# Building the S5 tables beside the FFN: output products on VectorE, a reordered table stage, paced gathers

## The chip, the cores and the metric

The kernel runs on one core of a Trainium2 chip. The metric is the device time of one execution in microseconds (us), the median of several runs. A core has five engines with their own instruction queues, each worked in order: TensorE (PE, with PEld for its weight loads), VectorE (DVE), ScalarE (ACT), GpSimd (POOL) and SyncE (SP), which here only issues DMAs. They meet through semaphores; data lie in SBUF (128 partitions) and in PSUM, into which TensorE writes.

## The reference

A decoder trunk of two layers with SEQ = 256 tokens and D_MODEL = 1024: in each layer a half-step SwiGLU FFN, a token mixer (layer 0: differential attention, layer 1: an S5 state-space block with GLU), a second half-step FFN, and a gated per-layer input (PLE). Every sub-layer has an RMSNorm before and behind it.

```
for i in range(DEPTH):
    x = x + 0.5 * rmsnorm(swiglu(rmsnorm(x, g[0]), ffn_w_in[i, 0], ffn_w_out[i, 0]), g[1])
    h = rmsnorm(x, g[2])
    m = diff_attention(h, ...) if i % 2 == 0 else s5_glu(h, ...)
    x = x + rmsnorm(m, g[3])
    x = x + 0.5 * rmsnorm(swiglu(rmsnorm(x, g[4]), ffn_w_in[i, 1], ffn_w_out[i, 1]), g[5])
    gate = sigmoid(rmsnorm(x, g[6]) @ ple_w_gate[i])
    x = x + rmsnorm(gate * (p[i] @ ple_w_proj[i]), g[7])
```

The S5 block is what the change is about. Each of 64 groups of 16 channels has 64 complex states, and the reference scans them:

```
lam_dt = lam * dt;  a_bar = exp(lam_dt);  b_bar = ((a_bar - 1) / lam) * b
a_pow  = exp(steps * lam_dt)
xs = associative_scan(a_bar, b_bar @ u) + a_pow * state
y  = real(c @ xs) + d_g * u
z  = gelu(y) @ w_glu + b_glu
```

The kernel doesn't scan token by token. It works in pieces of eight tokens with tables that depend only on the parameters: V (powers of a times b: from the inputs into the state), O (c times powers of a: from the state to the outputs), T (a block-Toeplitz table from inputs to outputs in one piece, the products c a^k b with d on its diagonal) and E (powers of a to the eighth, for the step from piece to piece).

## The kernel before

The 256 tokens are two row blocks of 128, worked by two threads (b = 0 and 1) whose steps alternate. The stages are ffn00, attn, ffn01, ple0, ffn10, ssm with GLU, ffn11, ple1. Matmuls keep fp32 accuracy by splitting: each product is a trio, hi*hi (L312), lo*hi (L313), hi*lo (L314). Weights come as blocks of 128x1024: SP loads raw (512 KB; three raw buffers), ACT rounds it to hi (L136), DVE subtracts to get lo (L138); nine pairs of hi and lo are held. Blocks are numbered in the order of their use: 100 to 143 are the first matrix of ffn01 (up), 144 to 165 its second (dn), 166 to 173 the PLE gate, 174 to 239 ffn10, and then come those of the S5 block.

Between two stages stand a post-norm (ygpn L383, the norm's factors v_pn and r_pn on POOL, x L387), then the transposes of x on PE (xT_ps, L349) with their split into xThi (ACT) and xTlo (DVE, L332).

The tables are built by a generator, ssm_tables, which thread b = 1 advances every few of its steps while ffn01, ple0 and the start of ffn10 run. Its parts are, in this order: a's powers and the complex multiplies (cmul, L717 to L726) of the E powers (10 of them, 60 DVE instructions, names cme, er, ei); b's and c's tables (names cmb, br, bi, cre, cim); and then for each of eight groups six POOL products of 128x512 for V (L907 to L912, names vr, vi, ptv), copies of c (cp), eight PE transposes (v_ps, L933) with an ACT copy and the store to v_d, eight small matmuls and a transpose for T (m_ps, L940 and L946), and six more POOL products for O (names or, oi, pto, in the same two buffers as vr and vi) with their stores o_d (L956). Then d is put on T's diagonal (db, dg, msb, L960 to L969), the pieces are stored to m_d (L972), and eight gathers of 512 KB in DRAM, issued by POOL, lay out the table t_d (L975).

Which instruction stands where on an engine is not decided by the chip: when the program is built, a scheduler plays the threads' steps through with priorities (the generator's steps get their own) and writes one order for each engine. On the chip every engine follows its list and waits where an input or a buffer isn't ready.

Of the kernel before, what the change touches and what calls it, by code (L numbers as in the profile page):

```python
# [9 lines left out]
F32 = mybir.dt.float32  # L10
# [3 lines left out]
ALU = mybir.AluOpType  # L14
AX = mybir.AxisListType

P = 128
# [50 lines left out]
          ("ffn", 1, 0), ("ssm",), ("ffn", 1, 1), ("ple", 1)]  # L68
TABLE_EVERY = OPT.get("every", 3)
PREPARE_AT = 36  # L70
EARLY = 24
# [76 lines left out]
def trunk(ctx, tc, x, p, norm_g, ffn_w_in, ffn_w_out, attn_w_qkv, attn_w_o, attn_lam, attn_subln_g,  # L148
# [136 lines left out]
    def flat(u):  # L285
        return [u] if isinstance(u, int) else [a for e in u for a in flat(e)]
# [479 lines left out]
    def ssm_tables(pool, keep):  # L766
# [61 lines left out]
        yield  # L828
        erf, eif = (t.rearrange("p g q j -> p (g q) j") for t in (er, ei))
        for m in (1, 2, 4, 8, 16):  # L830
            w = min(m, 31 - m)
            for h in range(2):
                sl = slice(16 * h, 16 * h + 16)
                b_r = erf[:, sl, m:m + 1].broadcast_to([P, 16, w])
                b_i = eif[:, sl, m:m + 1].broadcast_to([P, 16, w])
                cmul(v, pool, erf[:, sl, m + 1:m + w + 1], eif[:, sl, m + 1:m + w + 1], erf[:, sl, 1:w + 1], eif[:, sl, 1:w + 1],
                     b_r, b_i, [16, w], f"e{m}{h}")
            if m >= 4:
                yield

# [17 lines left out]
        for nm, src in (("re", ssm_b_re), ("im", ssm_b_im)):  # L858
            t = pool.tile([P, 32, 16], F32, tag="v" + nm[0], name=f"braw{nm}", bufs=1)
            nc.sync.dma_start(t, src[0].rearrange("(c e) p h -> (e p) c h", e=2))  # L860
            bb.append(t)
# [33 lines left out]
        cps = []  # L895
        for j in range(2):
# [6 lines left out]

        def products(out_r, out_i, ar_, ai_, br_, bi_, nm):
            g = nc.gpsimd
            t = pool.tile([P, 512], F32, tag="pt", name=f"pt{nm}", bufs=1).rearrange("p (q k h) -> p q k h", q=4, k=8)
# [7 lines left out]
        zt = pool.tile([16, 112], F32, tag="vr", name="zt", bufs=1)  # L914
        nc.gpsimd.memset(zt, 0.0)
        nc.gpsimd.dma_start(m_d[:, :, 0:7, :].rearrange("i g k o -> i g (k o)"),
                          zt.rearrange("p (o x) -> p o x", o=1).broadcast_to([16, 64, 112]))
        for gp in range(8):
            vr = pool.tile(shp, F32, tag="vr", name=f"vr{gp}", bufs=1)
            vi = pool.tile(shp, F32, tag="vi", name=f"vi{gp}", bufs=1)  # L920
            A = [t[:, :, gp, 0:8].broadcast_to(shp) for t in a4]
            B = [t[:, :, gp:gp + 1, :].broadcast_to(shp) for t in b4]
            products(vr, vi, *A, *B, f"v{gp}")
            for e in range(2):
                sl = slice(64 * e, 64 * e + 64)
                nc.gpsimd.tensor_copy(cps[0][sl, :, e, :], c_re[sl, :, gp, :])
                nc.gpsimd.tensor_scalar(cps[1][sl, :, e, :], c_im[sl, :, gp, :], -1.0, None, ALU.mult)
            for i in range(2):
# [9 lines left out]
            for ri in range(2):  # L938
                for q in range(4):
                    nc.tensor.matmul(mp[32 * q:32 * q + 32, 0:P], cps[ri][:, q].rearrange("p e h -> p (e h)"),  # L940
                                     (vr, vi)[ri][:, q].rearrange("p k h -> p (k h)"), start=ri == 0, stop=ri == 1,
                                     skip_group_check=True)
# [4 lines left out]
            nc.scalar.copy(msb[:, gp].rearrange("p e q h -> p q e h"), mp2[:, :P].rearrange("p (q e h) -> p q e h", q=4, e=2))  # L947
            yield
# [9 lines left out]
            yield  # L958

        m16 = msb.rearrange("p g e q h -> p (g e q) h")  # L960
        for q in range(4):
            db = pool.tile([16, 16, 16], F32, tag="cn", name=f"db{q}", bufs=1)
            nc.gpsimd.dma_start(db, ssm_d[:, 256 * q:256 * q + 256].rearrange("o (g h) -> o g h", h=16).broadcast_to([16, 16, 16]))
            dg = pool.tile([16, 16, 16], F32, tag="vi", name=f"dg{q}", bufs=1)
            nc.gpsimd.dma_start(dg, norm_g[1, 2:3, 256 * q:256 * q + 256].rearrange("o (g h) -> o g h", h=16).broadcast_to([16, 16, 16]))
            v.tensor_tensor(db, db, dg, ALU.mult)
            v.tensor_tensor(db, db, ident[0:16, 0:16].rearrange("p (o h) -> p o h", o=1).broadcast_to([16, 16, 16]), ALU.mult)
            mq = msb.rearrange("p g e q h -> p (g e) q h")[0:16, :, q, :]
            v.tensor_tensor(mq, mq, db, ALU.add)  # L969
        yield 1  # L970
        for k in range(8):
            nc.gpsimd.dma_start(m_d[:, :, 7 + k, :], m16[16 * k:16 * k + 16])  # L972
        yield 2
        for s_ in range(8):
            nc.gpsimd.dma_start(t_d[16 * s_:16 * s_ + 16].rearrange("i g (c x) -> i (g c) x", x=P),  # L975
                              m_d.rearrange("i g k o -> i g (k o)")[:, :, 16 * s_:16 * s_ + P])
            yield 2

# [309 lines left out]
    while any(s_ == "run" for s_ in state):  # L1288
# [16 lines left out]
        if started and b == 1 and steps[1] % pre["every"] == 0:  # L1305
            tables_step()
        if has_ssm and "pool" in ssm and ("V", 0) not in ssm and W.next >= plan[("ssm",)][0][0] - OPT["vl"]:
            load_v()
        if state == ["join", "join"]:
            end_tables()  # L1310
            if ("V", 0) not in ssm:
                load_v()
            pool = ssm["pool"]
# [30 lines left out]
```

## Time and profile before

| | us |
|---|---|
| median of 3 runs (lowest, highest) | 1120.79 (1118.37, 1122.93) |
| the profiled execution | 1120.96 |
| span from its first to its last instruction | 1119.2 |
| PE busy | 1043.0 (93%) |
| DVE busy | 696.5 (62%) |
| ACT busy | 553.8 (49%) |
| POOL busy | 255.4 (23%) |
| mean granted TensorE clock | 0.975 |

The profile is of one execution. Busy shares are averages over stages with different limits; POOL, for example, is busy 85 to 90% of the time from 420 to 616 us and hardly elsewhere. Times in the views are in us from the span's start. A view by windows gives the busy time of each engine in each stretch, with the granted clock (1.00 is full speed) and the DMA share. "Idle before" and "waited for" give idle time of an engine, put down to what ended it.

### The profile page before, as it was taken

How to read it: one execution, taken by the hardware profiler on the slowest of the kernel's cores; microseconds unless marked ns; L12 is line 12 of the kernel's file. 1: busy time of each engine (PE TensorE's matmuls, PEld its weight loads, DVE VectorE, ACT ScalarE, POOL GpSimd, SP SyncE). 2: the span in 40 equal slices, each digit the busy share in tenths (PEclk: the TensorE clock that was granted, in tenths of full speed). 3: DMA queues.
4: the chain of work that ended last, by engine and by line, in shares of the span. 5: the costliest groups of instructions: out<-in, count | busy, mean ns of one | idle time of the engine just before them, and what ended most of it. 6: DMA issues, size and time to landing. Idle time of an engine off the chain costs nothing. (4 is left out here: it accounts for less than half of the span.)

```text
span 1119.2 us, 14344 instructions
## 1 busy us (share of the span) xinstructions
PE 1043.0 (93%) x5123; PEld 835.7 (75%) x5123; DVE 696.5 (62%) x1011; ACT 553.8 (49%) x875; POOL 255.4 (23%) x315
## 2 busy tenths in 40 slices
PE   7999999999989999999778998999768899999996
PEld 5888888787766887777556886888546778888885
DVE  6656645688568986554686663654377676555464
ACT  6545444566655544443464543543335465444454
POOL 1002100100011018887788530000131010000001
PEclk9999999999999999999898999999989999999999
DMA  9656656476366777666564778766874647665651
GB/s 328 197 149 189 210 189 201 144 235 201 106 144 185 207 179 233 208 194 216 157 181 118 211 236 307 247 198 206 225 308 166 204 148 215 188 186 180 198 168 57
DMA packets 119816, 218.62 MB, mean 195 GB/s; under 512 B 25025, under 2 KB 43489, under 8 KB 119745
## 3 DMA queue, kind: packets, MB, share of 16 engines
q1 hardware_dynamic: 116864, 211.71, 60.9%
q0 software_dynamic: 1824, 5.33, 1.7%
q8 instruction: 40, 0.66, 0.2%
q10 hardware_dynamic: 1056, 0.66, 0.2%
q14 instruction: 32, 0.25, 0.1%
HBM read 205.13 MB, written 16.74 MB: 198 GB/s over the span
## 5 line engine op out<-in xcount | busy, mean ns | idle before, releaser
L138 DVE TENSOR_TENSOR lo<-raw,hi 128x1024 fp32r<-128x1024 f32 x332 | 429.6, 1301 | 266.3 <-ACT hi L136 264.7
L136 ACT CAST hi<-raw 128x1024 fp32r<-128x1024 f32 x332 | 347.3, 1052 | 327.1 <-PE up L314 106.5
L312 PE MATMUL up<-hi,xThi 128*128 128x512 f32 x704 | 279.3, 400 | 5.2 <-ACT hi L136 2.9
L313 PE MATMUL up<-lo,xThi 128*128 128x512 f32 x704 | 278.8, 397 | 1.5 <-DVE lo L138 1.4
L314 PE MATMUL up<-hi,xTlo 128*128 128x512 f32 x704 | 279.0, 400 | 0.0
L312 PEld LDWEIGHTS up<-hi,xThi 128*128 128x128 f32 x704 | 133.9, 190 | 34.8 <-ACT xThi L331 4.3
L313 PEld LDWEIGHTS up<-lo,xThi 128*128 128x128 f32 x704 | 134.1, 190 | 31.1 <-DVE lo L138 3.6
L314 PEld LDWEIGHTS up<-hi,xTlo 128*128 128x128 f32 x704 | 133.5, 191 | 28.1 <-issue 0.4
L312 PE MATMUL dn<-hi,hThi 128*128 128x512 f32 x352 | 139.2, 396 | 0.0
L313 PE MATMUL dn<-lo,hThi 128*128 128x512 f32 x352 | 138.5, 393 | 0.0
L314 PE MATMUL dn<-hi,hTlo 128*128 128x512 f32 x352 | 138.4, 394 | 0.0
L312 PEld LDWEIGHTS dn<-hi,hThi 128*128 128x128 f32 x352 | 66.8, 190 | 14.2 <-issue 0.6
L314 PEld LDWEIGHTS dn<-hi,hTlo 128*128 128x128 f32 x352 | 66.7, 190 | 14.3 <-issue 0.2
L313 PEld LDWEIGHTS dn<-lo,hThi 128*128 128x128 f32 x352 | 66.8, 190 | 13.6
L331 ACT ACTIVATE xThi<-xT_ps,gT 128x128 fp32r<-128x128 f32 x112 | 38.2, 368 | 59.2 <-PE xT_ps L349 58.3
L323 POOL TENSOR_SCALAR v_pn<-sspn,sspn 128x1 f32<-128x1 f32 x8 | 3.4, 422 | 246.8 <-ACT junkpn L380 244.7
L335 ACT CAST hThi<-hT_ps 128x512 fp32r<-128x512 f32 (+1 forms) x48 | 26.4, 550 | 56.2 <-PE hT_ps L459 56.0
L336 DVE TENSOR_TENSOR hTlo<-hT_ps,hThi 128x512 fp32r<-128x512 f32 (+1 forms) x48 | 30.8, 643 | 36.8 <-ACT hThi L335 36.7
L332 DVE SCALAR_TENSOR_TENSOR xTlo<-xT_ps,gT,xThi 128x128 fp32r<-128x128 f32 x112 | 36.1, 344 | 26.0 <-ACT xThi L331 25.5
L349 PE MATMUL xT_ps<-ident,x 128*128 128x128 f32 x112 | 30.3, 305 | 22.4 <-DVE xTlo L332 9.9
L349 PEld LDWEIGHTS xT_ps<-ident,x 128*128 128x128 f32 x112 | 16.2, 150 | 32.6 <-DVE xTlo L332 13.4
L456 DVE SCALAR_TENSOR_TENSOR h<-up,r_pre,sg 128x512 f32<-128x512 f32 (+1 forms) x48 | 33.6, 702 | 10.7 <-ACT sg L454 7.3
(360 smaller groups left out, 1319.5 us busy)
## 6 DMA issues: line engine op xcount, KB each, us to landing
raw<-in_ffn_w_in_dram SPq DMA_DIRECT2D x160, 512.0 KB, 4.4
raw<-in_ffn_w_out_dram SPq DMA_DIRECT2D x88, 512.0 KB, 3.9
raw<-in_attn_w_qkv_dram SPq DMA_DIRECT2D x24, 512.0 KB, 4.4
raw<-in_ffn_w_in_dram SPq DMA_DIRECT2D x32, 256.0 KB, 3.7
raw<-in_ple_w_gate_dram SPq DMA_DIRECT2D x16, 512.0 KB, 3.5
raw<-in_ssm_w_glu_dram SPq DMA_DIRECT2D x16, 512.0 KB, 4.1
gain<-in_norm_g_dram SPq DMA_DIRECT2D x8, 512.0 KB, 4.8
raw<-in_attn_w_o_dram SPq DMA_DIRECT2D x8, 512.0 KB, 4.2
```

Of the source, the lines that this page charges most:

```text
L136: nc.scalar.copy(hi, raw)
L138: (nc.gpsimd if n in self.on_pool else nc.vector).tensor_tensor(lo, raw, hi.bitcast(F32), ALU.subtract)
L312: nc.tensor.matmul(out_ap, st_hi, w_hi, start=start, stop=False)
L313: nc.tensor.matmul(out_ap, st_hi, w_lo, start=False, stop=False)
L314: nc.tensor.matmul(out_ap, st_lo, w_hi, start=False, stop=stop)
L323: nc.gpsimd.tensor_scalar(v, parts[0], parts[1], eps, ALU.add, ALU.add)
L331: return (nc.scalar.activation(hi, psum, AF.Copy, scale=scale).ins, nc.vector.scalar_tensor_tensor(lo, psum, scale, hi.bitcast(F32), ALU.m ...
L332: nc.vector.scalar_tensor_tensor(lo, psum, scale, hi.bitcast(F32), ALU.mult, ALU.subtract).ins)
L335: nc.scalar.copy(hi, psum)
L336: nc.vector.tensor_tensor(lo, psum, hi.bitcast(F32), ALU.subtract)
L349: marks[b].append(nc.tensor.transpose(pt, xb[:, k * P:(k + 1) * P], ident).ins)
L456: nc.vector.scalar_tensor_tensor(h[:, :w], up_, r, sg[:, :w], ALU.mult, ALU.mult)
```

## The change

- The 60 instructions of the E powers move from ahead of b's tables to behind the eight groups.
- The six products of O run on DVE (tile pto, tag pt) into buffers of their own, one each for or and oi; V's products stay on POOL with a scratch of their own (tag pv).
- vr and vi get two buffers, and cp two sets. The loop runs nine times, and the transposes and the T matmuls of group gp - 1 (function toeplitz) are written behind the products of group gp.
- The generator's last part waits until weight block 198 has been asked for. Then each of the eight gathers follows a 1x1 POOL copy that reads the newest hi tile (pace), with four thread steps between two of them.
- Four loads of V (512 KB each, ahead of the S5 stage) are issued one per step from 16 blocks ahead of that stage's first weights on, each behind the last raw load, where they stood together before.
- The region in which descriptors for POOL's DMAs are written is set to 4096 bytes.

```diff
-        erf, eif = (t.rearrange("p g q j -> p (g q) j") for t in (er, ei))
-        for m in (1, 2, 4, 8, 16):
-            ...  (the E powers; they come again, unchanged, behind the groups)
-        def products(out_r, out_i, ar_, ai_, br_, bi_, nm):
-            g = nc.gpsimd
-            t = pool.tile([P, 512], F32, tag="pt", name=f"pt{nm}", bufs=1).rearrange(...)
+        def products(g, tag, out_r, out_i, ar_, ai_, br_, bi_, nm):
+            t = pool.tile([P, 512], F32, tag=tag, name=f"pt{nm}", bufs=1).rearrange(...)
             g.tensor_tensor(out_r, ar_, br_, ALU.mult)
             g.tensor_tensor(t, ai_, bi_, ALU.mult)
             g.tensor_tensor(out_r, out_r, t, ALU.subtract)
...
-        for gp in range(8):
-            vr = pool.tile(shp, F32, tag="vr", name=f"vr{gp}", bufs=1)
-            vi = pool.tile(shp, F32, tag="vi", name=f"vi{gp}", bufs=1)
+        for gp in range(9):
+            if gp < 8:
+                vs_[gp] = vr, vi = [pool.tile(shp, F32, tag=t, name=f"{t}{gp}", bufs=2) for t in ("vr", "vi")]
...
+                products(nc.gpsimd, "pv", vr, vi, *A, *B, f"v{gp}")
+            if gp:
+                toeplitz(gp - 1, *vs_.pop(gp - 1))
+            yield 2
...
-            o_r = pool.tile(shp, F32, tag="vr", name=f"or{gp}", bufs=1)
-            o_i = pool.tile(shp, F32, tag="vi", name=f"oi{gp}", bufs=1)
+            o_r = pool.tile(shp, F32, tag="or", name=f"or{gp}", bufs=1)
+            o_i = pool.tile(shp, F32, tag="oi", name=f"oi{gp}", bufs=1)
...
-            products(o_r, o_i, *A, *C, f"o{gp}")
+            products(v, "pt", o_r, o_i, *A, *C, f"o{gp}")
...
-        yield 1
+        while W.next < flat(plan[("ffn", 1, 0)])[0] + TD_FROM:
+            yield 1
         for k in range(8):
             nc.gpsimd.dma_start(m_d[:, :, 7 + k, :], m16[16 * k:16 * k + 16])
         yield 2
+        pace = pool.tile([1, 8], F32, tag="zt", name="pace", bufs=1)
         for s_ in range(8):
-            nc.gpsimd.dma_start(t_d[...], m_d...)
-            yield 2
+            n = max(W.tiles)
+            gate = nc.gpsimd.tensor_copy(pace[:, s_:s_ + 1], W.tiles[n][0].bitcast(F32)[0:1, 0:1])
+            with tc.issue_after(gate.ins):
+              nc.gpsimd.dma_start(t_d[...], m_d...)
+            yield 4
...
             for j in range(2):
-                nc.sync.dma_start(ssm["V", pr][j], v_d[2 * pr + j])
+                with tc.issue_after(W.last_raw.ins):
+                    nc.sync.dma_start(ssm["V", pr][j], v_d[2 * pr + j])
+                yield
```

Lines of the kernel after stand two further on up to the E powers (lo is L140, the transposes of x are L351), and O's products are L897 to L902.

On DVE, at the weight blocks 124 and 125 of ffn01, the order before has the E powers (cme, er) and no products:

```order
492 L138 TENSOR_TENSOR lo124_3800<-raw124_3797,hi124_3799 128x1024
493 L719 TENSOR_TENSOR er_3298<-cme810_3448 128x16x8
494 L721 TENSOR_TENSOR cme812_3452<-er_3298,ei_3299 128x128
495 L722 TENSOR_TENSOR cme812_3452<-ei_3299,er_3298 128x128
496 L726 TENSOR_TENSOR ei_3299<-cme812_3452 128x16x8
497 L717 TENSOR_TENSOR cme1600_3493<-er_3298 128x240
498 L718 TENSOR_TENSOR cme1600_3493<-ei_3299 128x240
499 L138 TENSOR_TENSOR lo125_3869<-raw125_3866,hi125_3868 128x1024
```

The order after has the products of O's groups 2 and 3 there:

```order
474 L140 TENSOR_TENSOR lo125_3832<-raw125_3829,hi125_3831 128x1024
475 L898 TENSOR_TENSOR pto2_3959<-ai_3142,cim_3544 128x512
476 L899 TENSOR_TENSOR or2_3957<-or2_3957,pto2_3959 128x512
477 L900 TENSOR_TENSOR oi2_3958<-ai_3142,cre_3475 128x512
478 L140 TENSOR_TENSOR lo126_3862<-raw126_3859,hi126_3861 128x1024
479 L901 TENSOR_TENSOR pto2_3959<-ar_3141,cim_3544 128x512
480 L338 TENSOR_TENSOR hTlo011_3214<-hT_ps0111_3741,hThi011_3213 128x512
481 L458 SCALAR_TENSOR_TENSOR h0102_3849<-up01021_3706,r_pre040_3017,sg0102_3847 128x512
482 L902 TENSOR_TENSOR oi2_3958<-oi2_3958,pto2_3959 128x512
483 L897 TENSOR_TENSOR or3_4050<-ar_3141,cre_3475 128x512
484 L140 TENSOR_TENSOR lo127_3923<-raw127_3920,hi127_3922 128x1024
```

O's 48 products now stand among lo119 to lo137 (rows 452 to 528), and the E powers among lo138 to lo146 (rows 529 to 602).

On PE, at the start of the PLE gate (gtple, weight blocks 166 and 167), the order before still has table work of group 5 between the transposes of x:

```order
2195 L312 MATMUL gtple001_5243<-hi167_5175,xThi060_5207 128x512
2196 L313 MATMUL gtple001_5243<-lo167_5176,xThi060_5207 128x512
2197 L933 MATMUL v_ps50_4546<-ident_90,vr5_4532 128x128
2198 L940 MATMUL m_ps5_4561<-vr5_4532,cp0_3816 32x128 x4
2199 L349 MATMUL xT_ps0601_5210<-ident_90,x0_99 128x128
2200 L314 MATMUL gtple000_5242<-hi167_5175,xTlo060_5208 128x512
```

The order after has none there:

```order
2250 L314 MATMUL gtple001_5234<-hi167_5166,xThi060_5198 128x512
2251 L315 MATMUL gtple001_5234<-lo167_5167,xThi060_5198 128x512
2252 L351 MATMUL xT_ps0601_5201<-ident_90,x0_99 128x128
2253 L316 MATMUL gtple000_5233<-hi167_5166,xTlo060_5199 128x512
2254 L316 MATMUL gtple001_5234<-hi167_5166,xTlo060_5199 128x512
```

Its last table instruction on PE is row 2137, ahead of the first transpose of x for the PLE gate at row 2233; before, groups 5 to 7 stood behind that transpose (rows 2197 to 2439).

On POOL, the order before has the eight gathers in a row behind the diagonal's DMAs:

```order
210 L965 DMA dg3_4975<-in_norm_g_dram 16x256
211 L963 DMA db3_4973<-in_ssm_d_dram 16x256
212 L972 DMA m_d_111<-msb_3815 1024x1x16
213 L975 DMA t_d_113<-m_d_111 1024x128 x8
214 L1051 MEMSET zeros_7144 1x512
```

The order after puts a pace copy ahead of each, four weight blocks apart:

```order
170 L329 TENSOR_TENSOR r_pre101_5646<-v_pre101_5644,neg_half_95 128x1
171 L988 COPY pace_6023<-hi198_6007 1x1
172 L990 DMA t_d_113<-m_d_111 1024x128
173 L988 COPY pace_6023<-hi202_6095 1x1
174 L990 DMA t_d_113<-m_d_111 1024x128
175 L988 COPY pace_6023<-hi206_6182 1x1
```

The diagonal's DMAs and m_d stand ahead of row 152 there, which is the first norm factor (v_pn) behind ffn01.

## Rows read from the trace of the kernel before

**Rows 1.** Windows, L312 alone: window and length, PE busy (x count), PEld, clock, DMA
```profile
364.00:392.00 28.00, 15.41 (x40) 7.38 (x40) 1.00 0.70 207
...
420.00:532.00 112.00, 52.72 (x132) 25.30 (x133) 0.98 0.68 213
532.00:616.00 84.00, 31.24 (x70) 14.78 (x71) 0.88 0.52 150
...
672.00:700.00 28.00, 13.04 (x33) 6.22 (x32) 0.94 0.87 304
...
196.00:224.00 28.00, 14.16 (x35) 6.59 (x35) 1.00 0.47 145
```

**Rows 2.** Windows, all instructions: PE, PEld, DVE, ACT, POOL busy, clock, DMA, GB/s
```profile
420.00:532.00 112.00, 105.57 (x538) 82.40 (x537) 62.29 (x46) 47.65 (x64) 92.94 (x73) 0.98 0.68 213
532.00:616.00 84.00, 67.91 (x314) 49.78 (x314) 58.49 (x65) 44.58 (x88) 68.85 (x60) 0.88 0.52 150
```

**Rows 3.** Waits of PE, 420 to 616: us in total, times, longest
```profile
PE v_ps L933 <- POOL vi L912: 9.7, 5, 3.5
PE xT_ps L349 <- DVE xTlo L332: 8.6, 3, 3.7
PE xT_ps L349 <- DVE x L387: 3.8, 1, 3.8
```

**Rows 4.** Waits of ACT, 660 to 700
```profile
ACT hi L136 <- DMA raw<-in_ffn_w_in_dram: 24.4, 8, 9.6
```

**Rows 5.** Chain of waits: start, length, what
```profile
669.17 20.85 DMA raw<-in_ffn_w_in_dram
```

**Rows 6.** The tile t_d: duration in ns, first and last start
```profile
L975 POOL DMA_DIRECT2D t_d<-m_d x8: 757/757/772, 665.4 to 670.7; - x8
```

**Rows 7.** Timeline, 486 to 496: start, length, instruction
```profile
488.21 5.51 DVE L138 TENSOR_TENSOR lo<-raw,hi 128x1024 fp32r<-128x1024 f32 x3 [0.95 <-ACT hi L136]
...
488.42 2.17 POOL L912 TENSOR_TENSOR oi<-oi,pto 128x512 f32<-128x512 f32 x1
...
490.55 2.09 POOL L907 TENSOR_TENSOR vr<-ar,br 128x512 f32<-128x512 f32 x1
```

**Rows 8.** Groups of DVE, 420 to 616: busy, mean ns, idle before
```profile
L138 DVE TENSOR_TENSOR lo<-raw,hi 128x1024 fp32r<-128x1024 f32 x49 | 82.7, 1699 | 48.9 <-ACT hi L136 48.9
...
L383 DVE TENSOR_TENSOR ygpnple<-mple,gain 128x512 f32<-128x512 f32 x4 | 6.4, 1618 | 0.0
```

**Rows 9.** Timeline of DVE, 325 to 404, without POOL products
```profile
334.54 0.68 DVE L870 TENSOR_TENSOR brawre<-brawre,gb 128x512 f32<-128x512 f32 x1
335.13 0.68 DVE L870 TENSOR_TENSOR brawim<-brawim,gb 128x512 f32<-128x512 f32 x1
...
376.58 0.18 DVE L721 TENSOR_TENSOR cme<-er,ei 128x16 f32<-128x16 f32 x1
376.67 0.18 DVE L722 TENSOR_TENSOR cme<-ei,er 128x16 f32<-128x16 f32 x1
...
398.97 1.21 DVE L138 TENSOR_TENSOR lo<-raw,hi 128x1024 fp32r<-128x1024 f32 x1
400.10 0.40 DVE L717 TENSOR_TENSOR cme<-er 128x240 f32<-128x240 f32 x1
400.42 0.40 DVE L718 TENSOR_TENSOR cme<-ei 128x240 f32<-128x240 f32 x1
```

**Rows 10.** Timeline of POOL, 440 to 460: the copies of one group
```profile
452.81 0.51 POOL L926 COPY cp<-cre 64x64 f32<-64x64 f32 x2
453.38 0.80 POOL L927 TENSOR_SCALAR cp<-cim 64x64 f32<-64x64 f32 x2
```

**Rows 11.** Timeline, 378 to 386: weight block 119
```profile
378.99 1.22 DVE L138 TENSOR_TENSOR lo<-raw,hi 128x1024 fp32r<-128x1024 f32 x1
...
385.60 0.39 PE L313 MATMUL up<-lo,xThi 128*128 128x512 f32 x1
```

**Rows 12.** DMA issues: count, KB each, median us to landing
```profile
o_d<-or SPq DMA_DIRECT2D x16, 128.0 KB, 2.5
```

More of the change, by code (lines that the diff above doesn't have):

```diff
@@ L69 @@
 TABLE_EVERY = OPT.get("every", 3)
+V_AHEAD = 16
+TD_FROM = 24
 PREPARE_AT = 36
@@ L858, in ssm_tables @@
         for nm, src in (("re", ssm_b_re), ("im", ssm_b_im)):
-            t = pool.tile([P, 32, 16], F32, tag="v" + nm[0], name=f"braw{nm}", bufs=1)
+            t = pool.tile([P, 32, 16], F32, tag="o" + nm[0], name=f"braw{nm}", bufs=1)
             nc.sync.dma_start(t, src[0].rearrange("(c e) p h -> (e p) c h", e=2))
@@ L895, in ssm_tables @@
         cps = []
-        for j in range(2):
+        for j in range(4):
             cp = pool.tile([P, 4, 2, 16], F32, tag=f"cp{j}", name=f"cp{j}", bufs=1)
@@ L902, in ssm_tables @@
         shp = [P, 4, 8, 16]
[L904 to L906 removed]
+        def products(g, tag, out_r, out_i, ar_, ai_, br_, bi_, nm):
+            t = pool.tile([P, 512], F32, tag=tag, name=f"pt{nm}", bufs=1).rearrange("p (q k h) -> p q k h", q=4, k=8)
             g.tensor_tensor(out_r, ar_, br_, ALU.mult)
@@ L912, in products, with toeplitz @@
             g.tensor_tensor(out_i, out_i, t, ALU.add)
[L914 to L917, printed above, removed]
-        for gp in range(8):
-            vr = pool.tile(shp, F32, tag="vr", name=f"vr{gp}", bufs=1)
-            vi = pool.tile(shp, F32, tag="vi", name=f"vi{gp}", bufs=1)
[L921 to L927, printed above, removed]
+        def toeplitz(gp, vr, vi):
             for i in range(2):
@@ L939, in ssm_tables @@
                 for q in range(4):
-                    nc.tensor.matmul(mp[32 * q:32 * q + 32, 0:P], cps[ri][:, q].rearrange("p e h -> p (e h)"),
+                    nc.tensor.matmul(mp[32 * q:32 * q + 32, 0:P],
+                                     cps[2 * (gp % 2) + ri][:, q].rearrange("p e h -> p (e h)"),
                                      (vr, vi)[ri][:, q].rearrange("p k h -> p (k h)"), start=ri == 0, stop=ri == 1,
@@ L947, in ssm_tables @@
             nc.scalar.copy(msb[:, gp].rearrange("p e q h -> p q e h"), mp2[:, :P].rearrange("p (q e h) -> p q e h", q=4, e=2))
-            yield
-            o_r = pool.tile(shp, F32, tag="vr", name=f"or{gp}", bufs=1)
-            o_i = pool.tile(shp, F32, tag="vi", name=f"oi{gp}", bufs=1)
+        zt = pool.tile([16, 112], F32, tag="vr", name="zt", bufs=2)
+        nc.gpsimd.memset(zt, 0.0)
+        nc.gpsimd.dma_start(m_d[:, :, 0:7, :].rearrange("i g k o -> i g (k o)"),
+                          zt.rearrange("p (o x) -> p o x", o=1).broadcast_to([16, 64, 112]))
+        vs_ = {}
+        for gp in range(9):
+            if gp < 8:
+                vs_[gp] = vr, vi = [pool.tile(shp, F32, tag=t, name=f"{t}{gp}", bufs=2) for t in ("vr", "vi")]
+                for e in range(2):
+                    sl = slice(64 * e, 64 * e + 64)
+                    nc.gpsimd.tensor_copy(cps[2 * (gp % 2)][sl, :, e, :], c_re[sl, :, gp, :])
+                    nc.gpsimd.tensor_scalar(cps[2 * (gp % 2) + 1][sl, :, e, :], c_im[sl, :, gp, :], -1.0, None, ALU.mult)
+                A = [t[:, :, gp, 0:8].broadcast_to(shp) for t in a4]
+                B = [t[:, :, gp:gp + 1, :].broadcast_to(shp) for t in b4]
+                products(nc.gpsimd, "pv", vr, vi, *A, *B, f"v{gp}")
+            if gp:
+                toeplitz(gp - 1, *vs_.pop(gp - 1))
+            yield 2
+            if gp == 8:
+                continue
+            o_r = pool.tile(shp, F32, tag="or", name=f"or{gp}", bufs=1)
+            o_i = pool.tile(shp, F32, tag="oi", name=f"oi{gp}", bufs=1)
             A = [t[:, :, gp, 1:9].broadcast_to(shp) for t in a4]
             C = [t[:, :, gp:gp + 1, :].broadcast_to(shp) for t in cs]
-            products(o_r, o_i, *A, *C, f"o{gp}")
+            products(v, "pt", o_r, o_i, *A, *C, f"o{gp}")
             for e in range(2):
@@ L957, in ssm_tables @@
                                         t[64 * e:64 * e + 64].rearrange("p q t h -> p (q t h)"))
-            yield
+            yield 3
+        erf, eif = (t.rearrange("p g q j -> p (g q) j") for t in (er, ei))
+        for m in (1, 2, 4, 8, 16):
+            w = min(m, 31 - m)
+            for h in range(2):
+                sl = slice(16 * h, 16 * h + 16)
+                b_r = erf[:, sl, m:m + 1].broadcast_to([P, 16, w])
+                b_i = eif[:, sl, m:m + 1].broadcast_to([P, 16, w])
+                cmul(v, pool, erf[:, sl, m + 1:m + w + 1], eif[:, sl, m + 1:m + w + 1], erf[:, sl, 1:w + 1], eif[:, sl, 1:w + 1],
+                     b_r, b_i, [16, w], f"e{m}{h}")
+            if m >= 4:
+                yield
         m16 = msb.rearrange("p g e q h -> p (g e q) h")
@@ L963, in ssm_tables @@
             nc.gpsimd.dma_start(db, ssm_d[:, 256 * q:256 * q + 256].rearrange("o (g h) -> o g h", h=16).broadcast_to([16, 16, 16]))
-            dg = pool.tile([16, 16, 16], F32, tag="vi", name=f"dg{q}", bufs=1)
+            dg = pool.tile([16, 16, 16], F32, tag="pv", name=f"dg{q}", bufs=1)
             nc.gpsimd.dma_start(dg, norm_g[1, 2:3, 256 * q:256 * q + 256].rearrange("o (g h) -> o g h", h=16).broadcast_to([16, 16, 16]))
@@ L1306, in trunk @@
             tables_step()
-        if has_ssm and "pool" in ssm and ("V", 0) not in ssm and W.next >= plan[("ssm",)][0][0] - OPT["vl"]:
-            load_v()
+        if has_ssm and "pool" in ssm and b == 1 and W.next >= plan[("ssm",)][0][0] - V_AHEAD:
+            ssm.setdefault("loads", load_v())
+            next(ssm["loads"], None)
         if state == ["join", "join"]:
             end_tables()
-            if ("V", 0) not in ssm:
-                load_v()
+            for _ in ssm.setdefault("loads", load_v()):
+                pass
             pool = ssm["pool"]
```

14 lines of the change are left out of this document (3 added, 11 removed).

## The prediction

> **What bounds the kernel now.** I read first the counts of one matmul form by window [rows 1]. A weight block (128x1024) feeds four trios of matmuls, and L312 is the first of each trio, so its count is progress. At full rate 40 trios pass in 28 us, 0.70 us each, 2.8 us for a weight block. From 420 to 532, where the tables are built beside the FFN, 132 pass where 160 could: 28 x 0.70 = 19.6 us lost. From 532 to 616, the two changes of stage around the PLE gate with tables still running, 70 of 120: 35.0 us. From 672 to 700, 33 of 40: 4.9 us. A change of stage without tables (196 to 224) passes 35: 3.5 us. So some 50 us of this span hang on the tables, and they are lost for three reasons.
>
> Then the engines' busy time there [rows 2]: POOL works 93 of 112 us and 69 of 84, DVE only 62 of 112. In the second window the granted clock is 0.88 on the average, which is part of the 35 us. Then what PE waited for [rows 3]: the transposes of the table inputs on POOL's last product, 9.7 us, and the transposes of x on DVE's xTlo and x, 12.4 us; no wait for lo is among the causes. Last, the wait at 660 to 700 [rows 4 to 6]: ACT waits 24.4 us for raw weights, while POOL has issued eight gathers (t_d) between 665.4 and 670.7 and the chain of waits runs through one raw transfer of 20.85 us.
>
> **Part 1: the changes of stage are cleared.** In the new order the last table transpose stands on PE ahead of the PLE transposes of x, so all POOL and DVE products are ahead of them too. What leaves 532 to 616 is what distinguishes it from two clean changes: 35.0 - 2 x 3.5 = 28 us. The least that can be gained is the waits alone: 12.4 and the largest v_ps wait, 3.5, which falls there [rows 3], 16 us. I take 24, as the small diagonal multiplies (L966 to L969 of before) and the DMAs that POOL issues for them now stand inside the first change of stage, ahead of v_pn on POOL and among xTlo on DVE. Three groups of PE's table work leave here too; they are paid in part 3.
>
> **Part 2: gathers and V loads spread.** Each gather now waits for a newer hi tile, four blocks apart, and V loads go between raw loads. The bytes are the same. The 4.9 us of 672 to 700 go, if one gather at a time fits between the raws; I take all, with 0 (the same collisions, spread) and 6 as ends. A pace copy that waits holds POOL's queue, and behind it stand only the next gather and later norm sums.
>
> **Part 3: the table stretch.** Here the change adds. Of the 12 products of a group six go to DVE, 48 in all, and in DVE's order they stand between lo119 and lo137; the 60 E-power instructions follow, to lo146. So 28 weight blocks share DVE with 108 more instructions. In time of its own that would fit. What decides is whether DVE and POOL can work at once.
>
> The rows say they can't. With POOL products running, three lo take 5.51 us where a lone one steps on in 1.13, and the POOL products beside them take 2.17 and 2.09 [rows 7, 9]: they take turns, 1.13 for lo and so 2.15 - 1.13 = 1.03 for a product. A 128x512 multiply on DVE, the very size of the products that move, is 1618 ns on average beside POOL where one alone is 0.68 [rows 8, 9]. lo is 1699 ns there and still DVE has 48.9 us idle, so before there was room for the turns. The Trainium skill, in SBUF — State Buffer, section "Who interferes with whom", has it as a rule that speaks against this change: a VectorE instruction with two SBUF inputs and a GpSimd one that reads SBUF exclude each other for a whole instruction, and whoever comes first blocks the other. It would hold for every product and E power that moves here, and the trace agrees with it for lo and for the 128x512 multiply; no row of before has a VectorE product with the tables' broadcast operands beside POOL. By the rule the sum below stands; without it, it is that of the cheap rival.
>
> So I add the turns over lo119 to lo146. DVE's products: 48 x 0.60 (start to start of the two L870 [rows 9]) = 28.8. E powers: steps of 0.09 at the smallest width and 0.32 at the largest [rows 9], five widths of 12; at about 0.2, 12 us. lo: 28 x 1.13 = 31.6. POOL: a group is six products of 1.03 and four small copies, 0.51 + 0.80 for two pairs [rows 10], 7.5 us; seven of the eight groups fall here, since the two buffers let POOL run two groups ahead of PE: 52.5. Together 125 us. PE needs 28 x 2.8 = 78.4 in that time, so lo comes 46.6 late. lo's lead is used up first: lo119 ends at 380.21 and PE takes it at 385.60 [rows 11], 5.4. That leaves 41. PE's own table work is done in the gaps, but for the last two groups. Before, 4.5 groups cost 19.6 less the v_ps waits in that window (9.7 - 3.5 = 6.2), 13.4, so 3.0 each; two groups, 6. Loss 47.
>
> Bounds. With only six POOL groups inside (7.5 less), and POOL running under the 14 or so h and hTlo of the stretch, which read PSUM (about 0.7 each by the nearest size [rows 9], 10 us), 30. With all eight groups inside (7.5 more) and every E step at the 0.32 of the largest width (7 more), 61. From 30 to 61 I take 46, near the sum. The v_ps waits of before go, as POOL is ahead; but they are replaced by waits on lo, which is the wait that should appear. So the stretch changes by 46 - 19.6 = +26.4 (10 to 41).
>
> E powers in their old place cost PE nothing (40 trios from 364 to 392 [rows 1], as POOL had no products then); moving them later makes the products start earlier, and this is what lets part 1 happen, but it puts 12 us in a place without room.
>
> **Sum.** The profiled execution is 1120.96 us (span 1119.2 and 1.8 around it), 0.2 from the median 1120.79. 1120.96 - 24 - 4.9 + 26.4 = 1118.5 us. By the ends: 1120.96 - 28 - 6 + 10 = 1097, and 1120.96 - 16 - 0 + 41 = 1146. About half a percent, 5.6 us, is what a measurement of this kernel can tell from no change, so the forecast is no change, with the losses moved from the changes of stage into the FFN.
>
> **Rivals.** *Cheap products.* If turns are rarer than I count, because POOL, two groups ahead, waits for PE just when DVE multiplies, DVE's idle time takes the 28.8 + 12 us: it has 50 of 112 us free [rows 2]. Then PE loses only its table work, 8 x 3.0 = 24, +4.4 against before: 1120.96 + 4.4 - 24 - 4.9 = 1096 us. For it: no wait for lo in 420 to 616, in spite of POOL at 83%. Against: those idle times are waits on ACT's hi, thus time in which buffers were full; 2.5 products for each lo make it too little for turns.
>
> *Single buffers on the DVE queue: slower.* The output products have one buffer each for real and imaginary part, and the first product of a group overwrites what SP is still storing. A store takes 2.5 us to land [rows 12] after its issue, and SP's queue holds raw loads between, which wait for lo. If product and store follow without cover, DVE stands some 3 us in seven groups with every lo behind it: 21 us. It decides from the point where the turns no longer cover the store, that is where POOL has run out of buffers (two groups ahead) and DVE runs alone. For it: the store stands on SP behind a raw load that waits for a lo on the same DVE queue. Against: between a part's last product and its next use stand three to five instructions with their turns, 4 to 7 us. Then the time is 1118.5 + 21 = about 1139 us; half of it is 1129.
>
> *The gathers aren't cured.* If each gather still holds up one raw load, 4.9 us come back: 1123 us, still no change.
>
> **How the numbers follow.** The ledger's case (1108 to 1130) has 0.50, of which 0.15 lies below 1115.2, 0.27 within half a percent (the gathers' rival with it) and 0.08 above 1126.4. Cheap products (1085 to 1108) 0.27: the turns are well shown, but not how often both engines want the port. Single buffers, or the upper end of the turns (above 1130), 0.23. So faster 0.42, same 0.27, slower 0.31. The likeliest case's own range is 1108 to 1130; the range for 8 in 10 runs from 1096 to 1138, little inside the ends of the sum.
>
> **What would show it.** In the profile after: from about 380 to 500 the trios fall to some 25 in 28 us, with PE waiting on lo (L140) and DVE busy over 90%; lo and DVE's products with means well over 1.13 and 0.60; POOL's products near 2; then at the changes of stage 35 trios and no wait of xT on xTlo beyond 1 us; from 672 on 39 to 40 trios, and no raw transfer over 10 us. I am wrong if PE waits for lo less than 15 us in the table stretch (cheap products), if DVE waits for the o_d stores more than 10 us (single buffers), or if the changes of stage still lose over 20 us, since the diagonal multiplies then cost what the products did.

## The result and the profile after

The changed kernel takes 1126.23 us (median of 9 runs, 1123.01 to 1129.24), the kernel before 1120.66 beside it: a ratio of 1.0052, interval 1.0033 to 1.0070. It is slower by half a percent. Forecast were 1118.5 us and no change, 1096 to 1138. The time lies in that range; the forecast leaned the other way, and the interval lies wholly above 1. The profiled execution is 1125.46 us, its span 1123.6.

The windows of the same matmul form as in [rows 1] (it is L314 in the changed kernel), 40 trios being the full rate for 28 us:

```profile
364.00:392.00 28.00, 15.03 (x39) 7.16 (x39) 1.00 0.61 179
392.00:532.00 140.00, 54.06 (x126) 25.46 (x126) 0.90 0.63 186
532.00:616.00 84.00, 41.00 (x101) 19.40 (x101) 0.98 0.67 198
672.00:700.00 28.00, 15.34 (x40) 7.33 (x39) 1.00 0.76 242
```

The kernel before over the first long window, for comparison:

```profile
392.00:532.00 140.00, 67.91 (x171) 32.70 (x172) 0.99 0.68 207
```

| | trios short before | after | change, at 0.70 us | forecast |
|---|---|---|---|---|
| 392 to 532, table stretch | 29 | 74 | +31.5 us | +26.4 |
| 532 to 616, changes of stage | 50 | 19 | -21.7 | -24 |
| 672 to 700, gathers | 7 | 0 | -4.9 | -4.9 |
| sum | | | +4.9 | -2.5 |

The span grew by 4.4 us, near this sum, but the three places aren't the whole of it. Ahead of 392 us five trios (3.5 us) fewer have passed, and about as much comes back in the S5 stage, where executions of one kernel differ: from 784 to 868 us 49 trios pass in this profile and 44 in a second one of the same kernel (experiment 10, span 1127.4 us). All three parts went the way that was forecast; the one that costs was 5 us dearer, the ones that gain 2 us poorer, and between a gain of 29 and a cost of 26 that turned the sign.

The raw weights' wait of [rows 4] is gone (from 660 to 700 ACT waits for no raw weight), and the gathers, issued from 670 to 751 us instead of in one burst, land in 5.9 us on the median and 11.4 at most, where it took 11.2 and up to 19.5. From the view of the tile t_d, its issues and the times to landing:

```profile
L990 POOL DMA_DIRECT2D t_d<-m_d x8: 760/764/871, 670.2 to 750.9; - x8
...
DMA to landing us min/median/max: 5.0/5.9/11.4
```

The turns can be seen one by one. Timeline of the table stretch, DVE and POOL rows (start, length, instruction):

```profile
392.95 2.13 DVE L140 TENSOR_TENSOR lo<-raw,hi 128x1024 fp32r<-128x1024 f32 x1
394.07 2.15 POOL L902 TENSOR_TENSOR vi<-vi,ptv 128x512 f32<-128x512 f32 x1
395.00 1.77 DVE L901 TENSOR_TENSOR pto<-ar,cim 128x512 f32<-128x512 f32 x1
...
396.30 1.45 POOL L898 TENSOR_TENSOR ptv<-ai,bi 128x512 f32<-128x512 f32 x1
...
396.81 1.49 DVE L902 TENSOR_TENSOR oi<-oi,pto 128x512 f32<-128x512 f32 x1
...
397.83 1.59 POOL L899 TENSOR_TENSOR vr<-vr,ptv 128x512 f32<-128x512 f32 x1
398.22 2.28 DVE L140 TENSOR_TENSOR lo<-raw,hi 128x1024 fp32r<-128x1024 f32 x1
...
400.56 0.50 PE L315 MATMUL up<-lo,xThi 128*128 128x512 f32 x1 [2.38 <-DVE lo L140]
```

Read the ends: each DVE instruction ends about one POOL product (1.03 us in the prediction's count) and its own time after the one before it: 1.69 and 1.53 us for the two products, 2.20 for lo. A product with the tables' broadcast operands, which no row of before had beside POOL, takes 1.5 to 1.8 us here instead of 0.68. The Trainium skill's rule (SBUF — State Buffer, "Who interferes with whom") holds for it. At 400.56 PE has waited 2.38 us for lo.

It holds for small instructions too. Groups of DVE from 364 to 532 (busy, mean ns, idle before):

```profile
L140 DVE TENSOR_TENSOR lo<-raw,hi 128x1024 fp32r<-128x1024 f32 x44 | 63.3, 1439 | 9.2 <-ACT hi L138 9.2
L898 DVE TENSOR_TENSOR pto<-ai,cim 128x512 f32<-128x512 f32 x8 | 11.3, 1414 | 0.0
...
L900 DVE TENSOR_TENSOR oi<-ai,cre 128x512 f32<-128x512 f32 x8 | 8.2, 1024 | 2.5 <-DMA o_d<-oi 2.5
...
L721 DVE TENSOR_TENSOR er<-cme 128x16 f32<-128x16 f32 x2 | 1.3, 642 | 0.0
```

The two E powers of 128x16 in the last row take 642 ns on the mean, where one was 180 [rows 9]. It is a mean of two cases, without a product of POOL beside it and with one:

```profile
474.13 0.22 DVE L721 TENSOR_TENSOR er<-cme 128x16 f32<-128x16 f32 x1
...
475.16 1.12 POOL L897 TENSOR_TENSOR vr<-ar,br 128x512 f32<-128x512 f32 x1 [0.72 <-PE v_ps L911]
475.26 1.06 DVE L721 TENSOR_TENSOR er<-cme 128x16 f32<-128x16 f32 x1
```

DVE's idle time is nearly gone: 9.2 us for ACT's hi, 2.5 for the stores of oi and 0.2 for those of or. So the single buffers cost 2.7 us and not the 21 of that rival.

POOL's queue wasn't always full, though. Its waits from 392 to 532:

```profile
POOL cp L938 <- PE m_ps L918: 23.3, 3, 10.4
POOL vr L897 <- PE v_ps L911: 20.3, 6, 9.9
POOL cp L939 <- PE m_ps L918: 5.8, 3, 2.4
```

In these 49 us it waited for PE's table work, and DVE worked alone: 14 of the 48 output products ran with nothing of POOL beside them, and 26 took less than 0.8 us.

One sign that the prediction named failed, and is worth a look. PE's waits from 392 to 532:

```profile
PE hT_ps L461 <- DVE h L458: 9.0, 4, 4.4
PE up L315 <- DVE lo L140: 2.9, 2, 2.4
```

PE waits for lo only 2.9 us and for h, which stands in the same DVE queue, 9.0, though 51.8 us are lost. PE counts as busy for 128 of the 140 us, with 45 trios fewer than before. The list of waits alone would have said that the tables cost 12 us. Counting blocks through the trace (lo's in their order, four trios to a block) shows when each lo was ready and when PE first read it. At blocks 121 and 122 PE read it as it came. From block 124 to 147 it lay ready 3.5 to 15 us ahead, and between 408.3 and 480.7 us PE had no idle time at all. So for most of the stretch PE didn't stand waiting for a late lo; experiments 10 and 11 show what held it.

### The profile page after: what moved, and what is told of

It is laid out like the page before. It is cut to its first block, busy times and chain, and to the rows that moved or that the text cites. A ratio compares the mean times of both kernels' runs of the same rounds, so it can differ in the third digit from the quotient of the medians.

```text
span 1123.6 us, 14371 instructions
## 1 busy us (share of the span) xinstructions
PE 1054.7 (94%) x5123; PEld 839.9 (75%) x5123; DVE 731.4 (65%) x1059; ACT 554.8 (49%) x875; POOL 190.8 (17%) x277
## 4 chain that ended last, share of the span: by engine, by line
PE 55%; issue 21%; DVE 12%; DMA 6%; ACT 4%; POOL 1%; SPq 0%; DVEq 0%; POOLq 0%; ACTq 0%
PE up L315 9%; PE up L314 9%; PE up L316 9%; PE dn L315 4%; PE dn L316 4%; PE dn L314 4%; DVE lo L140 4%; DMA raw<-in_ffn_w_in_dram 3%; PE qkvat L314 2%; PE qkvat L315 2%; PE qkvat L316 2%; ACT hi L138 1%; PE hT_ps L461 1%; PE sp L598 1%; PE xT_ps L351 1%
## 5 line engine op out<-in xcount | busy, mean ns | idle before, releaser
L140 DVE TENSOR_TENSOR lo<-raw,hi 128x1024 fp32r<-128x1024 f32 x332 | 414.1, 1253 | 238.9 <-ACT hi L138 237.4
L314 PE MATMUL up<-hi,xThi 128*128 128x512 f32 x704 | 282.1, 403 | 6.4 <-ACT xThi L333 6.4
L315 PE MATMUL up<-lo,xThi 128*128 128x512 f32 x704 | 282.4, 403 | 3.4 <-DVE lo L140 3.3
L316 PE MATMUL up<-hi,xTlo 128*128 128x512 f32 x704 | 281.9, 405 | 0.0
L314 PEld LDWEIGHTS up<-hi,xThi 128*128 128x128 f32 x704 | 135.1, 192 | 37.3 <-ACT xThi L333 8.3
L314 PE MATMUL dn<-hi,hThi 128*128 128x512 f32 x352 | 138.0, 392 | 0.0
L314 PEld LDWEIGHTS dn<-hi,hThi 128*128 128x128 f32 x352 | 66.1, 188 | 13.4
L337 ACT CAST hThi<-hT_ps 128x512 fp32r<-128x512 f32 (+1 forms) x48 | 26.4, 551 | 63.7 <-PE hT_ps L461 63.6
L351 PE MATMUL xT_ps<-ident,x 128*128 128x128 f32 x112 | 29.7, 295 | 12.2 <-DMA x<-in_x_dram 5.0
L314 PE MATMUL qkvat<-hi,xThi 128*128 128x512 f32 x96 | 38.1, 397 | 0.3 <-ACT xThi L333 0.3
```

The lines of the kernel that those rows point to most:

```text
L140: (nc.gpsimd if n in self.on_pool else nc.vector).tensor_tensor(lo, raw, hi.bitcast(F32), ALU.subtract)
L314: nc.tensor.matmul(out_ap, st_hi, w_hi, start=start, stop=False)
L315: nc.tensor.matmul(out_ap, st_hi, w_lo, start=False, stop=False)
L316: nc.tensor.matmul(out_ap, st_lo, w_hi, start=False, stop=stop)
L337: nc.scalar.copy(hi, psum)
L351: marks[b].append(nc.tensor.transpose(pt, xb[:, k * P:(k + 1) * P], ident).ins)
```

## The experiments

Each is the changed kernel but for its edit, or another kernel where it says so. Ratios are against the kernel before on the same chip, with their intervals; its medians there were 1120.4 to 1122.7 us, so a few us between two experiments are better read from the ratios.

| | median us | ratio | trios short, 392 to 532 | 532 to 616 |
|---|---|---|---|---|
| changed kernel | 1126.23 | 1.0052 (1.0033 to 1.0070) | 74 | 19 |
| 1 output products and E powers late | 1104.98 | 0.9853 (0.9821 to 0.9884) | 31 | 28 |
| 2 E powers early | 1117.83 | 0.9970 (0.9954 to 0.9987) | 49 | 30 |
| 3 output products on POOL | 1133.72 | 1.0114 (1.0079 to 1.0149) | 68 | 28 |
| 4 before, with pacing | 1115.05 | 0.9942 (0.9923 to 0.9961) | 28 | 47 |
| 5 products gated | 1119.47 | 0.9988 (0.9967 to 1.0008) | 61 | 25 |
| 6 gated, no input products | 1105.03 | 0.9866 (0.9838 to 0.9894) | 35 | 18 |
| 7 as 1, diagonal late | 1103.93 | 0.9854 (0.9831 to 0.9876) | 31 | 22 |
| 8 as 7, late products on POOL | 1115.81 | 0.9950 (0.9929 to 0.9972) | 32 | 27 |
| 9 as 7, one buffer for vr and vi | 1116.79 | 0.9957 (0.9940 to 0.9973) | 8 | 43 |
| 10 changed kernel again | 1126.30 | 1.0053 (1.0032 to 1.0074) | 75 | 16 |
| 11 few table transposes | 1114.97 | 0.9933 (0.9906 to 0.9960) | 53 | 16 |

**1. Output products and E powers late.** They move behind the diagonal and are tied behind the newest lo:

```diff
+        while W.next < flat(plan[("ffn", 1, 0)])[0] + 8:
+            yield 1
+        for gp in range(8):
...
-            products(v, "pt", o_r, o_i, *A, *C, f"o{gp}")
+            with tc.issue_after(W.last_lo.ins):
+                products(v, "pt", o_r, o_i, *A, *C, f"o{gp}")
```

> As the changed kernel, but the output products and the E powers are issued late, in ffn10 (weight blocks 181 to 215), each group behind the newest lo; POOL has no products there. Theory of turns (DVE and POOL exclude each other on two SBUF operands): from 392 to 532 us only the input products share the port with lo, the loss falls from 51 us to PE's own table work, 24, and the 108 late instructions cost nothing, 39 to 40 trios per 28 us in ffn10: 1126.2 - 27 = about 1099 us. Rival (DVE's own time is what delays lo, with or without POOL): the loss moves along, ffn10 falls under 37 trios per 28 us, and the time stays at 1118 to 1126 us.

21 us less than the changed kernel, of 27 expected. The stretch passes 169 trios, and in ffn10 the same 108 instructions cost almost nothing: from 616 to 700, 117 of 120 trios pass.

```profile
392.00:532.00 140.00, 66.31 (x169) 31.69 (x169) 1.00 0.65 202
616.00:700.00 84.00, 45.55 (x117) 21.94 (x117) 1.00 0.82 251
```

The rival (DVE's own time) falls. The missing 6 us are in the change of stage, 28 trios short there instead of 19: PE waits 6.9 us once for x.

**2. E powers early.** The loop over m goes back to where it was.

> As the changed kernel, with the 60 instructions of the E powers back ahead of b's tables; output products on DVE stay. Theory of turns: 12 us of DVE's port time leave the contended stretch, the groups start some eight weight blocks later and end at block 161, still ahead of the change of stage: 1126.2 - 12 = about 1114 us. Rival (the 48 output products alone set the loss, the E powers fit into what is left): 1124 to 1128 us.

8 us less, of 12 expected. The stretch gains 25 trios (17.5 us), but the groups come later and the changes of stage lose 11 more (7.7 us). The rival falls.

**3. Output products on POOL.**

```diff
-            products(v, "pt", o_r, o_i, *A, *C, f"o{gp}")
+            products(nc.gpsimd, "pt", o_r, o_i, *A, *C, f"o{gp}")
```

> As the changed kernel, with the output products on POOL again. Theory of turns: the port's work grows by 48 x (1.03 - 0.60) = 20 us, lo gets its turns again, and PE waits for POOL's input products (v_ps) in place of lo; 1126 to 1140 us. Rival (DVE's own time): DVE is freed of 29 us, the loss from 392 to 532 falls to the 20 us of the kernel before, about 1101 us.

7.5 us more, in the range of the theory of turns, and the rival falls. Taking the work from DVE doesn't help while it stays in this place; PE now waits for POOL, 18.2 us in the stretch:

```profile
PE m_ps L918 <- POOL vr L899: 9.2, 4, 3.2
PE v_ps L911 <- POOL vi L902: 5.6, 1, 5.6
PE m_ps L918 <- POOL vi L902: 3.4, 2, 2.2
```

**4. The kernel before, with pacing.** Only the waiting loop, the pace copies and the spread loads of V are put into the kernel before.

> The kernel before with one part of the change alone: gathers behind a pace copy from weight block 198 on, and the loads of V spread between raw loads. The 4.9 us lost from 672 to 700 go and nothing else moves: 1120.7 - 4.9 = about 1116 us. Rival (the gathers take the same bandwidth wherever they are): 1120 to 1122 us.

A gain of 0.58%, 6.5 us (0.39 to 0.77%), where 4.9 were forecast; 40 trios pass from 672 to 700, and no other window moves by more than 3. This part of the change, gathers and loads of V together, is right by itself.

**5. Products gated.** The two lines with issue_after of experiment 1, in the products' place of the changed kernel.

> As the changed kernel, but each group of output products is issued behind the newest lo, so that products and E powers lie among lo120 to lo152 rather than lo118 to lo146. Control for the next run. Theory of turns: six more weight blocks share the work, each with 2.8 - 1.13 us of room: 1126.2 - 8 = about 1118 us. Rival (the first stall and the drop of the granted clock behind it set the loss, whatever the spacing): 1124 to 1128 us.

7 us less (8 expected): six more weight blocks for the same work. The rival falls.

**6. Gated, without POOL's input products.**

```diff
-                products(nc.gpsimd, "pv", vr, vi, *A, *B, f"v{gp}")
+                nc.gpsimd.memset(vr, 0.0)
+                nc.gpsimd.memset(vi, 0.0)
```

> The gated kernel without POOL's 48 input products: V's tables are filled with zeros by two memsets a group, so the table V and what follows from it are wrong. Output products and E powers stand at the same places on DVE, and PE's table work is the same. Theory of turns: without POOL beside them DVE's products step on in 0.60 us and lo in 1.13, PE loses only its own table work, under 24 us between 392 and 532: about 1095 us. Rival (DVE's own time delays lo, POOL or not): within 5 us of the gated kernel.

14 us less than the gated kernel, though DVE does the same work at the same places. DVE's groups from 392 to 532, and PE there:

```profile
L140 DVE TENSOR_TENSOR lo<-raw,hi 128x1024 fp32r<-128x1024 f32 x42 | 51.4, 1224 | 33.1 <-ACT hi L138 32.9
...
L898 DVE TENSOR_TENSOR pto<-ai,cim 128x512 f32<-128x512 f32 x8 | 5.5, 686 | 0.0
```

```profile
392.00:532.00 140.00, 140.00 (x715) 106.85 (x714) 102.34 (x169) 64.41 (x89) 20.98 (x35) 1.00 0.75 223
```

The products are at 686 ns, lo at 1224, DVE has 33 us idle, and PE is busy all the time at full clock. Still 35 trios are missing: 24.5 us, PE's own table work. Experiment 1 has 31 there (21.7 us) for all eight groups, so 22 to 25 us, near the 3.0 a group that the prediction had. The time, 1105, is 10 us above what was expected: 5.6 of it stand ahead of the window (group 0's zeros are ready early, its transposes go to where 97 trios pass from 252 to 364 instead of 105).

**7. Diagonal late.** db, dg and their multiplies go among the late products of experiment 1.

> The kernel with late output tables, and the diagonal of T late as well: its small DMAs (db, dg) and multiplies stand in ffn10 among the output products, not in the change of stage ahead of the PLE gate. In the run with late output tables PE waited 6.9 us there for x, while POOL and DVE waited for these DMAs with lo behind them. Theory: that wait and the late raw weights go, 1105 - 8 = about 1097 us. Rival (the post-norm itself takes that long, as its chain is serial): 1103 to 1106 us.

PE's wait for x is gone and the changes of stage gain 6 trios (4 us), yet the ratio is the same as that of experiment 1: the forecast missed, and the time is in the rival's range, though not for the rival's reason. PE reaches the S5 stage 5 us earlier in the profile and ends 1 us earlier: most is given back in or behind that stage. By what is open; two profiles of the changed kernel differ by as much there (49 and 44 trios from 784 to 868 us).

**8. The late output products on POOL.** As 7, with nc.gpsimd, each group behind a copy of a newer hi tile.

> The kernel with late output tables and diagonal, with the late output products on POOL, each group behind a 1x1 copy of a newer hi tile, in place of DVE. If the place decides and not the engine: as with DVE, about 1097 us, since POOL has nothing else in ffn10 and lo has room for turns (48 products of 1.03 us over some 24 weight blocks with 1.67 us of room each). If the engine decides (POOL's longer hold of the port): lo comes late in ffn10, 35 to 37 trios per 28 us there, 1102 to 1110 us.

12 us more than 7, and above the 1102 to 1110 us expected if the engine decides. From 616 to 700 100 trios pass instead of 118, lo goes from 1217 to 1469 ns:

```profile
616.00:700.00 84.00, 40.04 (x100) 19.21 (x100) 0.96 0.73 214
```

So the place alone doesn't decide. How much of the 12 us is the port is open, as the edit brings waits of its own: DVE stands 4.7 us for POOL's last product, whose scratch the E powers share (tag pt), and 3.2 us for db, each time with lo behind it.

**9. One buffer for vr and vi.** As 7, with bufs=1 and toeplitz(gp) right behind its products.

> The kernel with late output tables and diagonal, with one buffer for vr and vi and the transposes of a group right behind its products, as in the kernel before. In its order only group 0 stands ahead of the PLE gate's transposes of x, groups 1 to 7 stand at weight blocks 166 to 187, in the changes of stage. Theory (table work costs most where it meets a change of stage): the stretch up to 532 is nearly clean, but 532 to 616 loses 30 to 35 us as in the kernel before, where the kernel with two buffers loses about 15: PE's table work is the same 24 us, so 1104 + 10 to 15, about 1116 us. Rival (with the output products gone, POOL has room wherever the groups stand): 1100 to 1106 us.

13 us more than 7, as expected: the FFN is nearly clean (192 of 200), and 43 trios are short in the changes of stage and 22 more up to 672, where 7 has 22 and 2. So the second buffer and the later place of the transposes, which the run takes back together, bring the groups ahead of the change of stage, and that is worth 13 us (11 by the ratios) once the output products are out of the way.

**10. The changed kernel again.** The first profile has the granted clock at half (0.50, 1.2 GHz) for 17 us on end (408.8 to 425.9) behind PE's first waits. Was that the price?

> The changed kernel itself once more, for a second profile. Its first one has the granted clock at half from 402 to 426 us but for 3.4 us, behind the first waits for lo. If the half clock there is a part of the price of the first stall (theory), it comes again within a few us, and 392 to 448 pass some 40 trios again, where the gated kernel with a short spell passed 49. If it is chance, this profile has no such spell, and passes near 49 with a span some 6 us shorter.

No: the long spell didn't come, yet from 392 to 448 us 43 trios passed, against 40 and not 49. All instructions from 392 to 532, this run and then the changed kernel's first profile:

```profile
392.00:532.00 140.00, 122.58 (x593) 87.78 (x592) 127.04 (x158) 51.57 (x76) 82.13 (x69) 0.94 0.63 185
```

```profile
392.00:532.00 140.00, 128.17 (x601) 91.01 (x600) 125.81 (x157) 52.61 (x76) 80.42 (x68) 0.90 0.63 186
```

The granted clock is 0.94 instead of 0.90, so 5.6 us of half speed are missing; PE's idle time is 17.4 us instead of 11.8, 5.6 more; and 125 trios pass instead of 126. What PE doesn't lose to the half clock it loses waiting for h and lo. Both come from DVE's queue, and that queue took the same time in both profiles: 124.1 and 124.6 us from the end of lo119 to the end of lo147. That theory falls, and this also answers why the list of waits was so short: the 74 missing trios of the first profile are 11.8 us of idle PE, about 14 us lost to the half clock (0.10 x 140), and, as an estimate with the price of experiments 1 and 6, 22 to 25 us of table work, together 48 to 51 of 51.8 us.

**11. Few table transposes.** Two PE instructions a group instead of 17.

> The changed kernel with PE's table work cut from 17 instructions a group to 2 (one transpose of vr and one of vi, copied to all places of V's and T's tables, which are wrong so); all products on POOL and DVE stay, at places between those of the changed kernel and of the gated one (products to lo139, E powers to lo151). It asks for the step of the sum that is still open: does PE do its table work in the gaps that late lo leaves? If it does, as the prediction has it, the loss from 392 to 532 stays at what the turns alone cost, 35 to 41 us, and the time at 1114 to 1121 us. If the two add up, the loss is that of the changed and the gated kernel less the 24.5 us that PE lost without POOL's products, 18 to 27 us, and the time about 1100 us.

By its numbers the first case: 53 trios are missing, 37.1 us, and the time is 1115.0. So the turns alone cost about what the ledger has for them. But the loss didn't stay where it was: with the table work it was 51.8. And now PE shows what it waits for:

```profile
PE up L315 <- DVE lo L140: 16.7, 8, 4.0
PE dn L315 <- DVE lo L140: 3.3, 3, 1.5
PE hT_ps L461 <- DVE h L458: 2.2, 2, 1.7
```

It reads lo as it comes (within 0.3 us) at eleven of the blocks 119 to 147, where the changed kernel does at two. Fifteen of 17 instructions are some 20 us of the 22 to 25, an estimate by their number. Of these 14.7 come back against the changed kernel (51.8 - 37.1) and 5.6 against the gated one (42.7 - 37.1); the products' places lie between those of the two. So PE's table work is done in the gaps in part, by this run between a quarter and three quarters of it, and not all but the last two groups.

## Why the prediction was wrong

**Right: the mechanism, in the main.** DVE and POOL take turns on instructions with two SBUF operands, and DVE's queue with these turns bounds the table stretch: the same products on DVE take 0.69 us without POOL's beside them (experiment 6) and 0.8 to 1.4 on the mean with them, and without POOL's the time falls by 14 us. Each shift of the work to less crowded weight blocks gained two thirds or more of what was forecast (experiments 1, 2 and 5).

The ledger's 125 us for 28 lo came out too, 124.1 in the trace, but partly by luck. As POOL waited for PE's table work, its turns lengthened DVE's instructions by some 35 us and not 52.5 (an estimate: busy time of products, E powers and lo, less what they took without POOL). In its place stand the 15 h and hTlo of the stretch, 10 us of DVE that the ledger didn't count, and about 6 us of idle DVE. (The 1.03 us for a POOL product is 1.02 by its own difference, 2.15 - 1.13, and its two rows have 2.17 and 2.09; that changes nothing here.)

**Right: the gathers**, -4.9 us by the windows and -6.5 by the runs of experiment 4. **Nearly right: the changes of stage**, -21.7 instead of -24; the diagonal's share there was one wait of 6.9 us in the kernel of experiment 1, and in the changed kernel no wait of PE above 2.1.

**Wrong: the size of the table stretch's loss**, 51.8 us where "I take 46". The step that failed is "PE's own table work is done in the gaps, but for the last two groups", with "lo's lead is used up first" ahead of it: 41 us for 28 blocks and 6 behind them. Counted by blocks, PE lost 50.2 us from its first use of lo119 to that of lo147 (51.5 in the second profile), and 1.9 from there to block 165.

The ledger's 41 took lo's lead from 5.4 us to nothing. At lo119 it was 1.3, as the turns began ahead of it: POOL's first products start at 380.4 us, beside lo118 and the last of b's tables, and the first output product already stands ahead of lo119. And at lo147 the lead wasn't used up but 5.8 us again: PE was behind lo by then, with its own work, the table work of the groups that were to be free among it. These 4.1 and 5.8 us, less the 0.9 by which 124.1 is under 125, are the difference between 50.2 and 41.

Experiment 11 agrees: without most of the table work PE reads lo as it comes much more often, and 5.6 to 14.7 us come back. Why only a part fits into the gaps is not shown. Likely it is because PE works in order: a late lo or h holds up the transposes behind it, and only those that stand just ahead of it fall into its gap. The sum had no term for the half clock either (about 14 us in one profile, 8 in the other); by experiment 10 it changed nothing in the end. The table stretch is 5 of the 7 us between the forecast and the measured sum; 2 are from the changes of stage. The range from 30 to 61 for this term held it.

**The rivals.** Cheap products (0.27, 1085 to 1108 us) are out by the time, and DVE was busy for 125.8 of 140 us. Half of their mechanism came all the same: POOL did wait for PE while DVE multiplied. Single buffers (0.23) are out by 2.7 us of waits. The gathers were cured. What came is the ledger's own case, 1108 to 1130, and 1126.23 lies just under 1126.4, the border between its 0.27 for no change and its 0.08 above. With a gain of 29 and a cost of 26 worked out from unlike rows the sign of the sum was open; that the lean went to faster (0.42 against 0.31) had no row behind it but the middle of a wide range.

**A sign that misled:** "wrong if PE waits for lo less than 15 us (cheap products)". It waited 2.9, and the time was not that of cheap products. The sign took PE's table work as free; with most of it gone PE waits 20.0 us for lo (experiment 11). The count of trios is the sign that doesn't depend on how the lost time is booked.

**What the change should have been.** Two buffers for vr and vi, late transposes, pacing, and the output products and E powers on DVE, but in ffn10, where POOL has no products (experiments 1 and 7): 1104 us, 1.5% under the kernel before and 2% under the changed one, by the ratios 0.9853 and 1.0052.

## What to carry to other kernels

Moving elementwise work from GpSimd to VectorE gains little while the other engine still has work with two SBUF operands beside it: here 7.5 us in the same place (experiment 3), and 21 more, together with the E powers, in a stretch where POOL had no such work (experiment 1). Move it to a stretch where one of the two is idle, not to an engine that looks idle on the average. Count the shared port's work as one queue (products, lo and all) against what the consumer needs per unit of progress, and add the consumer's own extra work to it unless a run shows that it fits into the gaps. Measure a stretch by units of progress (here, trios of matmuls), since waits, slow clock and slower instructions change places in the books.

## What the runs showed of the hardware

Spells of half clock of TensorE cost nothing in the end here: with some 28 us at half clock or with 17 (0.90 and 0.94 of full over 140 us), 126 and 125 trios passed, since DVE's queue took the same time. The clock fell each time behind a wait of PE (2.38 us at 398.2, 2.65 at 405.6 and 4.39 at 480.7 in the first profile). While it was at half PE counted as busy throughout, with table work between the trios, and only 7 trios passed where 24 could:

```profile
408.84:425.90 17.06, 17.06 (x44) 8.86 (x44) 13.57 (x16) 3.33 (x5) 7.37 (x8) 0.50 0.74 227
```

And an instruction as small as 128x16 on VectorE pays a whole turn beside a GpSimd product, 1.06 us for 0.18; of the 60 E powers eleven took more than 0.8 us.
